# Two edits in a two-layer encoder: the inverse standard deviation by logarithm and exponential, and one accumulation pool for expansion and down projection

## The chip, the cores and the metric

The kernel runs on one core of a Trainium2 chip. The metric is the device time of one execution in microseconds (us). Before the change the median of three executions is 2300.8 us (2297.95 to 2302.07). A change of 0.2% is 4.6 us.

The engines that matter are TensorE (PE: matrix products, with the loading of weights into it listed apart as PEld), VectorE (DVE), ScalarE (ACT), and the transfers (DMA), which SyncE (SP) issues. TensorE writes its sums into PSUM, a small memory of eight banks; DVE and ACT read them from there.

## The reference, cut to what matters

Two layers act on 1056 tokens (1024 of a prompt and 32 of a sample, sharing the weights), with a model width of 1024 and an inner width D_FF of 2816:

```
x <- LN(alpha * x + mixer(x))
x <- LN(alpha * x + SwiGLU(x))              # (silu(x @ w1) * (x @ w3)) @ w2
x <- x + (p[i] @ W_ple) * sigmoid(x @ W_gate)

def layer_norm(x, g, b, eps=1e-5):
    mu = jnp.mean(xf, -1, keepdims=True)
    var = jnp.mean(jnp.square(xf - mu), -1, keepdims=True)
    return ((xf - mu) * lax.rsqrt(var + eps) * g + b)
```

The mixers (causal pooling and a gated convolution in layer 0, a token MLP and a state-space scan in layer 1) are not touched by the change. Everything is float32.

## The kernel before

**Arithmetic.** A float32 product is made of three reduced-precision products: each operand is split into a high part (an ACT copy, line 93 for weights and 411 for activations) and a low part (a DVE subtraction, lines 94 and 412), and high*high, low*high and high*low are accumulated. So every weight that a DMA brings costs one ACT and one DVE instruction before TensorE may use it.

**Stages of a layer.** The mixer; `tail`, which makes the output projection (lines 314 to 316) in token chunks of 384, 384 and 288 and normalises each chunk (first norm of the layer), then the first units of the expansion; `up`, the expansion by w1 and w3; `final`, the down projection by w2 (line 1448); `embed`, which makes the embedding products (line 1555), the gate's products (line 1576) and the second norm, in two token halves of 528.

**The expansion.** The 2816 inner columns are worked in groups g. For each g and each of w1 and w3 there is a *block* of seven outer products in place of eight (a one-level Strassen scheme, `mixed`). An outer product is 24 matmuls of 264 columns (line 1236) into a *quad*, a PSUM tile of two banks. From g = 3 on, in 32 blocks (eight g, w1 and w3, two layers), one of the seven outer products, number 2 for w1 or 4 for w3, is itself made by seven *inner pieces* of six matmuls each (`within`, from line 1140; matmuls at line 1153). Inner pieces 1, 6, 7, 4 use one bank, called u (tile `ia`), and pieces 2, 5, 3 another, called v (tile `ib`). After each piece a DVE addition (line 1164) or an ACT copy (line 1162) takes its sum out; pieces 6, 7, 4 and 3 then go on accumulating into a bank that has been read and is kept. The block's order is fixed by generator steps: pieces 1 and 2, then 5 and 6, then 3 and 7, then 4, with outer products asked for in between.

**PSUM.** `up` has a pool of its own: three quads (`q`) and the tiles `ia` and `ib`, 3*2 + 1 + 1 = 8 banks. It is closed after `up`, and a new pool of four quads is opened for `final` and `embed`. `final` takes all four quads at once (its first four are the four row blocks of one output product). Tiles of a pool are recycled in turn, and a wait for a tile's earlier reader is kept for the tile as a whole.

**The norm.** `norm` (line 1647) is cut into steps, each of which is put off by an amount of TensorE work, so that it runs while products go on: `first` (mean), `second` (variance, then the ACT square root at line 1685), `third` (DVE reciprocal at line 1690, ACT square at 1691), `fourth` and `fifth` (one Newton step at lines 1697 to 1703), then four `pieces` of two of the eight feature blocks (DVE multiplication at line 1709, ACT scale and shift at 1711, then the split 411/412). `minus` (line 1673) subtracts the mean from two feature blocks. There are ten norms in all: three chunks and two halves in each layer.

**The order of the work.** The program is written in one order, and a scheduler with its own model of durations then sets the order of instructions on each engine; on the chip every engine takes its instructions strictly in that order, and waits by semaphores.

Of the kernel before, what the change touches and what calls it, by code (L numbers as in the profile page):

```python
# [9 lines left out]
AF = mybir.ActivationFunctionType  # L10
ALU = mybir.AluOpType
PSUM = bass.MemoryType.PSUM
# [21 lines left out]
LN_A, LN_B, LN_C, LN_D, LN_S = 4.0, 2.0, 2.0, 4.0, 1.0  # L34
# [250 lines left out]
class Kernel:  # L285
# [50 lines left out]
    def build(self):  # L336
        nc, tc, a = self.nc, self.tc, self.a
        with ExitStack() as ctx:
            const = ctx.enter_context(tc.tile_pool(name="const", bufs=1))
            dram = ctx.enter_context(tc.tile_pool(name="dram", bufs=1, space=DRAM))  # L340
            ring = ctx.enter_context(tc.tile_pool(name="ring", bufs=1, side="right"))
            self.w = Weights(nc, ring, plan(a, self.steps, self.ple, self.inner))

            self.const = const
            self.operand("in")

            mp = ctx.enter_context(ExitStack())
            self.mp = mp.enter_context(tc.tile_pool(name="mix0", bufs=1, reuse_waits="tile"))
            xraw = self.mp.tile([P, KD, T], F32, tag="yf", name="xraw")


            xin = a["xT"]
            (t0, n) = CH[0]
            nc.sync.dma_start(out=xraw[:, 0:2, t0:t0 + n], in_=xin[:, 0:2, t0:t0 + n])
            self.w.prefetch()
            for c, (t0, n) in enumerate(CH):
                for k in range(0 if c else 2, KD, 2):
                    nc.sync.dma_start(out=xraw[:, k:k + 2, t0:t0 + n], in_=xin[:, k:k + 2, t0:t0 + n])
            cst = const.tile([P, 3 * P + 64], F32, name="cst")
            nc.sync.dma_start(out=cst, in_=a["cst"])  # L360
            self.ident, self.tri, self.ones = (cst[:, i * P:(i + 1) * P] for i in range(3))
            self.inv = cst[:, 3 * P:3 * P + 64].rearrange("p (g t) -> p g t", g=4)
            prm = const.tile([P, 124], F32, name="prm")
            nc.sync.dma_start(out=prm, in_=a["prm"])
            self.ln = prm[:, 0:64].rearrange("p (l s m) -> p l s m", l=4, s=2)
            self.pscale = prm[:, 64:68]
            self.cw = prm[:, 68:80].rearrange("p (k m) -> p k m", k=3)
            self.scw = prm[:, 80:112].rearrange("p (k m) -> p k m", k=4)
            self.scb = prm[:, 112:120]
            self.nw = prm[:, 120:124]  # L370
            self.mhalf = const.tile([P, 8], F32, name="mhalf")
            nc.vector.memset(self.mhalf, -0.5)
            nc.vector.tensor_scalar(out=self.ones, in0=self.ones, scalar1=1.0 / D, scalar2=None, op0=ALU.mult)
            for c in range(3):
                for k in range(0, KD, 2):
                    self.split(self.x[c], slice(k, k + 2), xraw[:, k:k + 2, CH[c][0]:CH[c][0] + CH[c][1]])

            self.spill = dram.tile([P, KD, T], F32, name="spill")
            self.resid = dram.tile([P, KD, T], F32, name="resid")
            self.acd = dram.tile([72, P], F32, name="acd")  # L380

            self.hidden = [dram.tile([P, 2, 2, NG, TH], F32, name=f"hidden{i}") for i in range(2)]
            for layer in range(2):
                if layer == 0:
                    self.layer0_mixer(self.x, xraw)
                    mp.close()
                else:
                    self.layer1_mixer(self.x)
                with ExitStack() as stack:
                    self.hp = stack.enter_context(tc.tile_pool(name=f"h{layer}", bufs=1, reuse_waits="tile"))  # L390
                    self.w.temps, self.w.temp_bufs = self.hp, 5
                    self.tail(layer)
                    self.tp = stack.enter_context(tc.tile_pool(name=f"t{layer}", bufs=1, reuse_waits="tile"))
                    with tc.tile_pool(name=f"psu{layer}", bufs=1, space=PSUM, reuse_waits="tile") as self.psum:
                        self.psum_bufs = {"q": 3, "ia": 1, "ib": 1}
                        self.up(layer)
                    self.psum = stack.enter_context(
                        tc.tile_pool(name=f"psb{layer}", bufs=1, space=PSUM, reuse_waits="tile")
                    )
                    self.psum_bufs = {"q": 4}  # L400
                    self.final(layer)
                    self.embed(layer)

# [736 lines left out]
    def within(self, layer, j, g):  # L1140


        nc, q, d, x = self.nc, TH // 2, self.sh, self.inside[j]
        m, t = {2: (0, 0), 4: (1, 0)}[j]
        (w,) = self.w.get(("in", layer, g, j))

        def bank(tag):
            return self.bank(tag)[:, :q]

        def one(ps, i, add):  # L1150
            for k in range(2):
                for c, (p, r) in enumerate(((0, 0), (1, 0), (0, 1))):
                    nc.tensor.matmul(  # L1153
                        ps, w[i][p][:, k * P:(k + 1) * P], x[i][r][:, k, :],
                        start=not add and k == 0 and c == 0, stop=k == 1 and c == 2, skip_group_check=add,
                    )
            self.passed(6 * q)

        def to(a, b, ps, new=False):
            o = d[a][:, m, t * TH + b * q:t * TH + (b + 1) * q]  # L1160
            if new:
                nc.scalar.activation(o, ps, AF.Copy)
            else:
                nc.vector.tensor_tensor(o, o, ps, op=ALU.add)

        u = bank("ia")
        one(u, 1, False)
        to(0, 0, u)
        v = bank("ib")
        one(v, 2, False)  # L1170
        to(0, 0, v)
        yield
        v = bank("ib")
        one(v, 5, False)
        to(1, 1, v, True)
        one(u, 6, True)
        to(0, 1, u)
        yield
        one(v, 3, True)
        to(0, 1, v)  # L1180
        one(u, 7, True)
        to(1, 1, u)
        yield
        one(u, 4, True)
        to(1, 0, u, True)
        yield
# [460 lines left out]
    def norm(self, ln, c, S, acc, x, n, done, wait=LN_A, rows=None):  # L1647
# [3 lines left out]
        nc, lp = self.nc, self.hp if rows else self.lp  # L1651
        if rows:
            mean, var, inv, tmp = (r[:, :n] for r in rows[:4])
        else:
# [3 lines left out]
            var, tmp = S[0][:, 1, :], S[0][:, 0, :]  # L1658
# [12 lines left out]
        def minus(k):  # L1671
            z = acc[:, k:k + 2, :]
            nc.vector.tensor_tensor(z, z, mean.unsqueeze(1).to_broadcast([P, 2, n]), op=ALU.subtract)
# [7 lines left out]
        def second():  # L1681
            ps, cut = average(S[1])
            nc.vector.tensor_tensor(cut(var), ps, cut(tmp), op=ALU.subtract)
            nc.vector.tensor_scalar(out=var, in0=var, scalar1=0.0, scalar2=EPS, op0=ALU.max, op1=ALU.add)
            nc.scalar.activation(tmp, var, AF.Sqrt)
            minus(0)
            self.defer(LN_B, third)

        def third():
            nc.vector.reciprocal(inv, tmp)  # L1690
            nc.scalar.activation(tmp, inv, AF.Square)
            minus(2)
            self.defer(LN_B, fourth)

        def fourth():

            nc.vector.tensor_tensor(tmp, tmp, var, op=ALU.mult)
            nc.scalar.activation(tmp, tmp, AF.Copy, scale=-0.5, bias=1.5)
            minus(4)
            self.defer(LN_B, fifth)  # L1700

        def fifth():
            nc.vector.tensor_tensor(inv, inv, tmp, op=ALU.mult)
            pieces(0)

        def pieces(k):
            ks = slice(k, k + 2)
            z = acc[:, ks, :]
            nc.vector.tensor_tensor(z, z, inv.unsqueeze(1).to_broadcast([P, 2, n]), op=ALU.mult)
            for kk in (k, k + 1):  # L1710
                nc.scalar.activation(
                    acc[:, kk, :], acc[:, kk, :], AF.Identity,
                    scale=self.ln[:, ln, 0, kk:kk + 1], bias=self.ln[:, ln, 1, kk:kk + 1],
                )
            if k == 0:
                minus(6)
            self.split(x, ks, z)
            done[c] += 1
            if k + 2 < KD:
                self.defer(LN_D if rows else LN_C, lambda: pieces(k + 2))  # L1720
# [118 lines left out]
```

## Time and profile before

| what | value |
|---|---|
| median of the executions shown | 2300.8 us (2297.95 to 2302.07) |
| profiled execution, own time | 2300.83 us |
| profiled execution, span of its trace | 2298.6 us |
| TensorE busy | 2270.4 us (99%) |
| VectorE busy | 1736.9 us (76%) |
| ScalarE busy | 1060.7 us (46%) |
| data moved | 241.46 MB, mean 105 GB/s |

A row of the profile's groups reads: line, engine, operation, output<-input with shapes, number of instructions | busy us, mean ns of one | idle time of the engine just before them, and what ended it. A row of the waits reads: engine, what it was to write and its line <- the engine, tensor and line that it waited for: total us, times, longest us. A row of the windows reads: from:to, length, then the busy time (and number) of PE, PEld, DVE, ACT, POOL, the granted TensorE clock (1.00 is full), the DMA share and GB/s. A row of the timeline reads: start, duration, engine, line, operation, count, and in brackets the idle time before it and its releaser.

### The profile page before, as it was taken

How to read it: one execution, taken by the hardware profiler on the slowest of the kernel's cores; microseconds unless marked ns; L12 is line 12 of the kernel's file. 1: busy time of each engine (PE TensorE's matmuls, PEld its weight loads, DVE VectorE, ACT ScalarE, POOL GpSimd, SP SyncE). 2: the span in 40 equal slices, each digit the busy share in tenths (PEclk: the TensorE clock that was granted, in tenths of full speed). 3: DMA queues.
4: the chain of work that ended last, by engine and by line, in shares of the span. 5: the costliest groups of instructions: out<-in, count | busy, mean ns of one | idle time of the engine just before them, and what ended most of it. 6: DMA issues, size and time to landing. Idle time of an engine off the chain costs nothing.

```text
span 2298.6 us, 41143 instructions
## 1 busy us (share of the span) xinstructions
PE 2270.4 (99%) x17183; PEld 2236.8 (97%) x17183; DVE 1736.9 (76%) x2820; ACT 1060.7 (46%) x1783; POOL 32.5 (1%) x40
## 2 busy tenths in 40 slices
PE   9999999999999999999999999999999999999998
PEld 8999989999999999999999989999999999999998
DVE  8755798977776788896656774898977776888893
ACT  5432464434443443584542662464444443434581
POOL 0000000000000000000000120000000000000000
PEclk9999999999999999999999999999999999999999
DMA  4113133333334632034211222142332335631132
GB/s 143 55 56 113 56 140 102 107 116 107 107 116 162 255 121 70 28 102 139 84 38 57 102 67 72 38 154 96 123 111 94 112 107 204 256 106 42 47 105 91
DMA packets 96478, 241.46 MB, mean 105 GB/s; under 512 B 12092, under 2 KB 21508, under 8 KB 94244
## 3 DMA queue, kind: packets, MB, share of 16 engines
q1 hardware_dynamic: 95524, 238.15, 30.5%
q8 instruction: 134, 2.20, 0.4%
q10 hardware_dynamic: 768, 0.68, 0.1%
q14 instruction: 52, 0.43, 0.1%
HBM read 196.99 MB, written 41.81 MB: 104 GB/s over the span
## 4 chain that ended last, share of the span: by engine, by line
PE 88%; DVE 7%; DMA 2%; ACT 2%; issue 1%; SPq 0%; POOL 0%; POOLq 0%; ACTq 0%
PE q L1236 28%; PE q L1448 20%; PE q L1576 8%; PE mm L314 6%; PE mm L315 6%; PE mm L316 6%; PE ia L1153 4%; PE ib L1153 3%; PE q L1555 2%; DVE bf L99 1%; PE mm L727 1%; PE mm L728 1%; PE mm L729 1%; DVE w L94 1%; DMA raw<-w 1%; PE ms L863 1%
## 5 line engine op out<-in xcount | busy, mean ns | idle before, releaser
L1448 PE MATMUL q<-w 128*128 128x264 f32 x3696 | 459.1, 286 | 4.3 <-DVE c_all L1254 2.2
L1448 PEld LDWEIGHTS q<-w 128*128 128x128 f32 x3696 | 457.8, 189 | 4.9 <-ACT w L93 4.7
L93 ACT ACTIVATE w<-bf 128x512 fp32r<-128x512 f32 (+1 forms) x314 | 184.5, 626 | 190.2 <-issue 69.1
L94 DVE TENSOR_TENSOR w<-raw,w 128x512 fp32r<-128x512 f32 (+2 forms) x182 | 171.2, 946 | 97.7 <-ACT w L93 97.5
L94 DVE TENSOR_TENSOR w<-bf,w 128x512 fp32r<-128x512 f32 (+1 forms) x314 | 207.0, 687 | 37.7 <-ACT w L93 37.3
L93 ACT ACTIVATE w<-raw 128x512 fp32r<-128x512 f32 (+2 forms) x182 | 149.1, 828 | 163.9 <-PE mm L316 75.2
L314 PE MATMUL mm<-xhgate,w 128*128 128x384 f32 (+1 forms) x576 | 188.6, 327 | 4.7 <-ACT xhgate L411 4.7
L1236 PE MATMUL q<-xhin,w 128*128 128x264 f32 x1152 | 188.3, 285 | 0.6 <-ACT u L481 0.6
L316 PE MATMUL mm<-xlgate,w 128*128 128x384 f32 (+1 forms) x576 | 186.6, 325 | 0.8 <-DVE xlgate L412 0.8
L315 PE MATMUL mm<-xhgate,w 128*128 128x384 f32 (+1 forms) x576 | 187.1, 325 | 0.0
L1576 PE MATMUL q<-xhgate,w 128*128 128x264 f32 x1024 | 167.1, 285 | 0.0
L1236 PEld LDWEIGHTS q<-xhin,w 128*128 128x128 f32 x1152 | 159.5, 188 | 1.5 <-ACT u L481 0.8
L1576 PEld LDWEIGHTS q<-xhgate,w 128*128 128x128 f32 x1024 | 142.0, 188 | 0.3
L314 PE MATMUL mm<-xhin,w 128*128 128x384 f32 (+1 forms) x384 | 127.4, 332 | 7.8 <-ACT xhin L411 5.6
L315 PE MATMUL mm<-xhin,w 128*128 128x384 f32 (+1 forms) x384 | 126.1, 329 | 0.6 <-DVE w L94 0.6
L316 PE MATMUL mm<-xlin,w 128*128 128x384 f32 (+1 forms) x384 | 125.7, 329 | 0.1
L1236 PE MATMUL q<-xhgate,w 128*128 128x264 f32 x768 | 125.3, 285 | 0.3 <-ACT xhgate L1204 0.2
L1236 PE MATMUL q<-t3sum,w 128*128 128x264 f32 x960 | 124.3, 285 | 0.0
L1236 PE MATMUL q<-t1sum,w 128*128 128x264 f32 x960 | 124.0, 285 | 0.0
L1236 PE MATMUL q<-t2sum,w 128*128 128x264 f32 x960 | 123.6, 284 | 0.0
L1236 PEld LDWEIGHTS q<-t1sum,w 128*128 128x128 f32 x960 | 120.3, 189 | 0.0
L1236 PEld LDWEIGHTS q<-t3sum,w 128*128 128x128 f32 x960 | 120.0, 189 | 0.0
(431 smaller groups left out, 4801.9 us busy)
## 6 DMA issues: line engine op xcount, KB each, us to landing
raw<-w SPq DMA_DIRECT2D x116, 512.0 KB, 3.7
hidden<-c_all SPq DMA_DIRECT2D x72, 264.0 KB, 2.1
rawx<-w SPq DMA_DIRECT2D x64, 256.0 KB, 2.9
raw<-w_gate SPq DMA_DIRECT2D x32, 512.0 KB, 3.6
raw<-w_in SPq DMA_DIRECT2D x16, 512.0 KB, 3.8
raw<-w_out SPq DMA_DIRECT2D x16, 512.0 KB, 3.5
xhdown<-hidden SPq DMA_DIRECT2D x12, 528.0 KB, 13.6
resid<-stream SPq DMA_DIRECT2D x4, 1056.0 KB, 4.9
```

The source lines that it names most:

```text
L93: self.nc.scalar.activation(hi, x, AF.Copy)
L94: self.nc.vector.tensor_tensor(lo, x, hi.bitcast(F32), op=ALU.subtract)
L99: self.nc.vector.tensor_tensor(t, a, b, op=op)
L314: nc.tensor.matmul(ps, wh, xh, start=first, stop=False)
L315: nc.tensor.matmul(ps, wl, xh, start=False, stop=False)
L316: nc.tensor.matmul(ps, wh, xl, start=False, stop=last)
L727: nc.tensor.matmul(o, xh, hi[:, s], start=k == 0, stop=False)
L1153: nc.tensor.matmul(ps, w[i][p][:, k * P:(k + 1) * P], x[i][r][:, k, :], start=not add and k == 0 and c == 0, stop=k == 1 and c == 2, skip_ ...
L1236: nc.tensor.matmul(ps[:, a, :TH // 2], w[q][:, ks], x[r][:, k, a * TH // 2:(a + 1) * TH // 2], start=not add and k == 0 and j == 0, stop=k ...
L1448: nc.tensor.matmul(ps[m][:, a, :TH // 2], v[q][:, ms], x[r][:, a * TH // 2:(a + 1) * TH // 2], start=j == 0 and n == 0, stop=j == NG - 1 a ...
L1555: nc.tensor.matmul(ps[:, b, :TH // 2], w[q][:, o:o + P], pe[k][r][:, t * TH + b * TH // 2:t * TH + (b + 1) * TH // 2], start=k == 0 and i ...
L1576: nc.tensor.matmul(ps[:, b, :TH // 2], w[q][:, ks], token_half((self.xh, self.xl), k, t, b)[r], start=k == 0 and i == 0, stop=k == KD - 1 ...
```

## The change

Two edits are made together.

1. *One pool.* The pool of four quads that `final` used is now opened before `up`, and both use it. The tiles `ia` and `ib` are gone; `within` takes one quad and uses its two banks as u and v. All seven pieces of an inner product then lie in one tile.
2. *The norm.* `second` now computes ln(var), exp(-0.5 ln(var)) and its square, three ACT activations in a row; the DVE reciprocal is gone. The Newton step follows in `third`, the last multiplication in `fourth`, and there is no `fifth`. The mean's subtractions `minus(4)` and `minus(6)` move from `fourth` and from the first of the `pieces` into the first two `pieces`, each behind that piece's multiplication.

```diff
@@ the program
                     self.tp = stack.enter_context(tc.tile_pool(name=f"t{layer}", bufs=1, reuse_waits="tile"))
-                    with tc.tile_pool(name=f"psu{layer}", bufs=1, space=PSUM, reuse_waits="tile") as self.psum:
-                        self.psum_bufs = {"q": 3, "ia": 1, "ib": 1}
-                        self.up(layer)
                     self.psum = stack.enter_context(
                         tc.tile_pool(name=f"psb{layer}", bufs=1, space=PSUM, reuse_waits="tile")
                     )
                     self.psum_bufs = {"q": 4}
+                    self.up(layer)
                     self.final(layer)
@@ within
-        def bank(tag):
-            return self.bank(tag)[:, :q]
-
@@
-        u = bank("ia")
+        ps = self.quads()
+        u, v = (ps[:, a, :q] for a in range(2))
         one(u, 1, False)
         to(0, 0, u)
-        v = bank("ib")
         one(v, 2, False)
         to(0, 0, v)
         yield
-        v = bank("ib")
         one(v, 5, False)
@@ norm
-            nc.scalar.activation(tmp, var, AF.Sqrt)
+            nc.scalar.activation(tmp, var, AF.Ln)
+            nc.scalar.activation(inv, tmp, AF.Exp, scale=-0.5)
+            nc.scalar.activation(tmp, inv, AF.Square)
             minus(0)
             self.defer(LN_B, third)

         def third():
-            nc.vector.reciprocal(inv, tmp)
-            nc.scalar.activation(tmp, inv, AF.Square)
+
+            nc.vector.tensor_tensor(tmp, tmp, var, op=ALU.mult)
+            nc.scalar.activation(tmp, tmp, AF.Copy, scale=-0.5, bias=1.5)
             minus(2)
             self.defer(LN_B, fourth)

         def fourth():
-
-            nc.vector.tensor_tensor(tmp, tmp, var, op=ALU.mult)
-            nc.scalar.activation(tmp, tmp, AF.Copy, scale=-0.5, bias=1.5)
-            minus(4)
-            self.defer(LN_B, fifth)
-
-        def fifth():
             nc.vector.tensor_tensor(inv, inv, tmp, op=ALU.mult)
             pieces(0)
@@ pieces
-            if k == 0:
-                minus(6)
+            if k < 4:
+                minus(k + 4)
             self.split(x, ks, z)
```

The scheduler sets a new order from this, which the diff does not show. Line numbers of the changed program are six or so lower: 1153 becomes 1148, 1164 becomes 1159, 1162 becomes 1157, 1236 becomes 1230, 1448 becomes 1442, 1685 becomes 1679.

**TensorE in a block with inner pieces.** Rows at line 1153 (before) or 1148 (after) are the inner pieces, the other rows are outer products; a count behind a row stands for so many matmuls. Before, for a w1 block, from piece 5 on (`ib` with an inner sum), through piece 6 (`ia`), 24 outer matmuls, piece 3 (five rows at `ib`) and piece 7 (`ia`):

```order
L1153 MATMUL ib_4787<-inner_3945,w_4586 128x264 [waits DVE_49]
L1153 MATMUL ib_4787<-inner_3945,w_4586 128x264 x5
L1153 MATMUL ia_4739<-inner_3945,w_4586 128x264 x6
L1236 MATMUL q_4704<-t2sum_3227,w_4701 128x264 [waits Activation_49]
L1236 MATMUL q_4704<-t2sum_3227,w_4701 128x264 x23
L1153 MATMUL ib_4787<-xhin,w_4586 128x264 [waits Activation_49]
L1153 MATMUL ib_4787<-xhin,w_4586 128x264
L1153 MATMUL ib_4787<-xlin,w_4586 128x264
L1153 MATMUL ib_4787<-xhin,w_4586 128x264 x2
L1153 MATMUL ib_4787<-xlin,w_4586 128x264
L1153 MATMUL ia_4739<-inner_3945,w_4586 128x264 [waits DVE_49]
L1153 MATMUL ia_4739<-inner_3945,w_4586 128x264 x5
```

The changed program, for a w3 block, from the last outer matmuls ahead of piece 5 to the first of piece 3:

```order
L1230 MATMUL q_4921<-t2sum_3227,w_4887 128x264 x4
L1148 MATMUL q_4958<-inner_3945,w_4807 128x264 [waits DVE_49]
L1148 MATMUL q_4958<-inner_3945,w_4807 128x264 x5
L1230 MATMUL q_4921<-t2sum_3227,w_4887 128x264 x4
L1148 MATMUL q_4958<-inner_3945,w_4807 128x264 [waits Activation_49]
L1148 MATMUL q_4958<-inner_3945,w_4807 128x264 x5
L1230 MATMUL q_4921<-t2sum_3227,w_4887 128x264 x16
L1148 MATMUL q_4958<-xhin,w_4807 128x264 [waits DVE_49]
```

Before, piece 6 followed piece 5 with no wait. After, all pieces write one tile, q_4958, and each waits for the reader of the piece before it: piece 6 for the ACT copy of piece 5, with four outer matmuls in between. Counted in the same way over the whole block, the outer matmuls between the pieces are, for a w1 block of the changed program, 1 (8) 2 (16) 5 (10) 6 (14) 3 (5) 7 (19) 4, and for a w3 block 1 (20) 2 (8) 5 (4) 6 (16) 3 (9) 7 (15) 4. The reader is an ACT copy behind pieces 5 and 4 and a DVE addition behind the others. All blocks of a kind from g = 3 on repeat this. The number of matmuls is the same in both programs.

**TensorE where the expansion ends and the down projection begins** (layer 0). Before:

```order
L1236 MATMUL q_7639<-t3sum_3228,w_7669 128x264 [waits Activation_49]
L1236 MATMUL q_7639<-t3sum_3228,w_7669 128x264 x23
L1448 MATMUL q_7873<-w_7779 128x264 [waits DVE_49,PE_49,Activation_49]
L1448 MATMUL q_7873<-w_7779 128x264 x5
```

After:

```order
L1230 MATMUL q_7609<-t3sum_3228,w_7639 128x264 [waits Activation_49]
L1230 MATMUL q_7609<-t3sum_3228,w_7639 128x264 x23
L1442 MATMUL q_7837<-w_7747 128x264 [waits PE_49,Activation_49]
L1442 MATMUL q_7837<-w_7747 128x264
L1442 MATMUL q_7837<-w_7747 128x264 [waits DVE_49]
L1442 MATMUL q_7837<-w_7747 128x264 x3
```

Before, the first down matmul waits for the readers of the last expansion product q_7639 (DVE), since the new pool's first quad lies on the old pool's banks. After, the first quad is one that had been read long since; its DVE wait is now for the low part of the weight. The wait for the readers of q_7609 stands at the fourth quad, 36 matmuls later.

**ScalarE in a norm** (first chunk of layer 0). Before:

```order
L1685 ACT_TABLE_LOAD [waits DVE_49]
L1685 ACTIVATE S_0_1_2422<-S_0_1_2422 128x384 [waits Activation_49]
L1691 ACTIVATE S_0_1_2422<-dg_0_0_2492 128x384 [waits DVE_49]
```

After:

```order
L1679 ACT_TABLE_LOAD [waits DVE_49]
L1679 ACTIVATE S_0_1_2422<-S_0_1_2422 128x384 [waits Activation_49]
L1680 ACT_TABLE_LOAD
L1680 ACTIVATE dg_0_0_2492<-S_0_1_2422 128x384 [waits Activation_49]
L1681 ACTIVATE S_0_1_2422<-dg_0_0_2492 128x384 [waits Activation_49]
```

The logarithm and the exponential each come with a load of their function table. Over the program VectorE loses ten instructions (the reciprocals), and ScalarE gains ten activations and twelve table loads.

## The prediction

> **What bounds the kernel now.** I read the page's totals first, then a window over `up` and over two of its blocks, since a stage's limit is not the mean's.
>
> ```profile
> PE 2270.4 (99%) x17183; PEld 2236.8 (97%) x17183; DVE 1736.9 (76%) x2820; ACT 1060.7 (46%) x1783; POOL 32.5 (1%) x40
> 430.00:733.00 303.00, 303.00 (x2484) 303.00 (x2483) 219.62 (x400) 129.68 (x231) 0.00 (x0) 1.00 0.32 110
> 441.60:461.27 19.67, 19.67 (x164) 19.67 (x163) 16.23 (x31) 9.09 (x17) 0.00 (x0) 1.00 0.27 96
> ```
>
> TensorE is busy 99% of the span. In layer 0's inner blocks it has no idle time at all at a clock of 1.00: 303.00 of 303.00 us, 303.00/2484 = 0.122 us a matmul. DVE (219.62) and ACT (129.68) have room. So here any wait put before a matmul lengthens the program one to one, and work taken from DVE or ACT gives nothing. Time can be won only where TensorE does wait, which the list of waits shows:
>
> ```profile
> PE mm L314 <- ACT xhin L411: 5.6, 2, 4.4
> PE mm L314 <- ACT xhgate L411: 4.7, 2, 4.4
> PE q L1448 <- DVE c_all L1254: 2.2, 1, 2.2
> PE q L1448 <- ACT w L93: 2.1, 1, 2.1
> PE q L1555 <- ACT t1down L1560: 0.3, 2, 0.2
> ```
>
> Two of these places belong to the change: 5.6 + 4.7 us at the first norm in `tail`, and 2.2 + 2.1 us where `final` begins.
>
> **Term 1: the inner pieces, +16.8 us.** Each of seven pieces now waits for the reader of the piece before it, because both banks are one tile; the order of the program shows six such waits a block, with few outer matmuls between some. What a round trip costs is read from one passage of the timeline in layer 0 and from the groups:
>
> ```profile
> 649.34 0.90 PE L1153 MATMUL ib<-inner,w 128*128 128x264 f32 x6
> 650.28 0.39 ACT L1162 ACTIVATE c_all<-ib 128x264 f32<-128x264 f32 x1
> ```
>
> ```profile
> L1153 PE MATMUL ib<-inner,w x192: 280/285/317, 432.8 to 1929.2; 128*128 128x264 f32 x192
> L1164 DVE TENSOR_TENSOR s_all<-s_all,ia 128x264 f32<-128x264 f32 x64 | 27.2, 424 | 54.1 <-PE ia L1153 54.1
> L1162 ACT ACTIVATE c_all<-ib 128x264 f32<-128x264 f32 x32 | 12.4, 387 | 2.5 <-PE ib L1153 0.6
> L93 ACT ACTIVATE w<-rawx 128x1024 fp32r<-128x1024 f32 x16 | 16.8, 1048 | 0.0
> L1251 ACT ACTIVATE s_all<-q 128x528 f32<-128x528 f32 x70 | 42.6, 608 | 128.1 <-PE q L1236 128.1
> L94 DVE TENSOR_TENSOR w<-bf,w 128x512 fp32r<-128x512 f32 (+1 forms) x314 | 207.0, 687 | 37.7 <-ACT w L93 37.3
> ```
>
> The six matmuls end at 650.24, the copy starts at 650.28: a hop of 0.04 us. A matmul lasts 0.285 us, the copy 0.39, the DVE addition 0.42. The way back is seen where TensorE waited for ACT in `tail`:
>
> ```profile
> 1490.32 0.44 PE L314 MATMUL mm<-xhgate,w 128*128 128x384 f32 x1 [0.27 <-ACT xhgate L411]
> 1490.60 0.34 PE L315 MATMUL mm<-xhgate,w 128*128 128x384 f32 x1
> 1490.77 0.34 PE L314 MATMUL mm<-xhgate,w 128*128 128x384 f32 x1
> ...
> 1497.49 0.83 ACT L411 ACTIVATE xhgate<-stream0b 128x768 fp32r<-128x768 f32 x1
> 1498.37 0.29 PEld L314 LDWEIGHTS mm<-xhgate,w 128*128 128x128 f32 x1 [4.75 <-ACT xhgate L411]
> 1498.37 0.69 PE L314 MATMUL mm<-xhgate,w 128*128 128x384 f32 x1 [4.43 <-ACT xhgate L411]
> ```
>
> ACT ends at 1498.32 and TensorE goes on at 1498.37: 0.05. There the weights were not loaded ahead (both rows start together). What that costs is seen at full clock at 1490.32: the next matmul starts 0.28 us later where 0.17 is usual, 0.11 more. From the start of a piece's last matmul to the next piece's first useful slot that is 0.285 + 0.04 + 0.39 + 0.05 + 0.11 = 0.88 us by ACT, 0.91 by DVE. With m outer matmuls between, the next would start after (m + 1) * 0.122, so seven or more cover the trip if the reader finds its engine free.
>
> Short by this alone are two waits in a pair of blocks: w1's 3 to 7 (m = 5, 0.73 us: 0.18) and w3's 5 to 6 (m = 4, 0.61 us: 0.27). By a queue ahead of the reader, three more. In w1's 5 to 6 (m = 10, 1.95 us from piece 5's first matmul) ACT has first a copy of 0.61 out of the outer product that ends just before piece 5, then a weight split of 1.05, then the piece's copy. With starts 0.1 us closer than durations, that ends at 0.2 + 0.5 + 0.95 + 0.39 = 2.04, and with 0.16 back it is 2.2: short by 0.3. In w3's 3 to 7 (m = 9) and 2 to 5 (m = 8) a DVE weight split can stand ahead of the addition; DVE is busy 16.23 of 19.67 us in a block, so it often will. One such split of 0.69 us leaves 0.91 + 0.69 against 1.22 and 1.10, short by 0.4 and 0.5 when it has only just begun and by nothing when it is nearly done; I take half of the first, 0.2, and, since behind piece 2 its weight's high part must come from ACT first, 0.1 for the second. The rest have 14 to 20. A pair thus loses 0.18 + 0.27 + 0.3 + 0.2 + 0.1 = 1.05 us; eight groups in two layers are 16 pairs, 16.8. Bounds: readers always at once, 0.45 * 16 = 7.2; at every second of the five short places half a DVE addition of 0.42 more, 16.8 + 16 * 2.5 * 0.21 = 25.2.
>
> The Trainium skill, "PSUM — Partial Sum Buffer", section "PSUM bank collisions raise a hardware error", says that PSUM has to be guarded by bank, so the two banks need no guard between them; by that rule the term would be nothing. The program's order puts the waits there all the same.
>
> **Term 2: the start of `final`, -5.7 us.**
>
> ```profile
> 737.98 3.08 PE L1236 MATMUL q<-t3sum,w 128*128 128x264 f32 x24
> 738.51 2.75 DVE L94 TENSOR_TENSOR w<-t2down,w 128x528 fp32r<-128x528 f32 x4 [0.31 <-ACT w L93]
> 741.80 1.31 DVE L1254 TENSOR_TENSOR c_all<-c_all,q 128x528 f32<-128x528 f32 x2
> 743.26 7.00 PE L1448 MATMUL q<-w 128*128 128x264 f32 x43 [2.20 <-DVE c_all L1254]
> 743.20:747.00 3.80, 3.74 (x19) 3.77 (x20) 3.59 (x6) 0.26 (x1) 0.00 (x0) 0.57 0.97 319
> 1943.20:1947.00 3.80, 3.73 (x30) 3.76 (x31) 3.60 (x6) 0.00 (x0) 0.00 (x0) 1.00 0.97 277
> ```
>
> The new pool's first quad waits for the last expansion product's readers, which stand behind four weight splits on DVE. After, that quad is wanted 36 matmuls, 4.4 us, later, and the first weights' low parts (from 738.51) are mostly there when TensorE comes, at the end of its last outer product near 741.1. Gone are 2.2 and 2.1 us of waits, and in layer 0 the low clock behind it: 19 matmuls in 3.74 us where layer 1 at 1.00 has 30, a loss of 11 * 0.124 = 1.4. Sum -5.7. It is 0 if the low part of the weight arrives as late as the readers did; more than -5.7 there isn't.
>
> **Term 3: the first norm, -2.6 us.**
>
> ```profile
> 1488.67 2.54 DVE L1690 RECIPROCAL dg<-S 128x384 f32<-128x384 f32 x1
> 1494.88 0.95 DVE L1709 TENSOR_TENSOR stream0b<-stream0b,dg 128x768 f32<-128x768 f32 x1
> ...
> 1498.85 0.52 PE L315 MATMUL mm<-xhgate,w 128*128 128x384 f32 x1
> 1499.17 0.52 PE L314 MATMUL mm<-xhgate,w 128*128 128x384 f32 x1
> 296.00:303.00 7.00, 4.59 (x15) 4.37 (x15) 7.00 (x11) 4.71 (x7) 0.00 (x0) 0.54 0.24 75
> 1497.80:1502.00 4.20, 3.63 (x13) 3.55 (x14) 4.20 (x7) 2.86 (x4) 0.00 (x0) 0.59 0.35 125
> L1690 DVE RECIPROCAL dg<-S 128x384 f32<-128x384 f32 x4 | 10.2, 2544 | 0.6 <-ACT S L1685 0.6
> L1685 ACT ACT_TABLE_LOAD x8 | 10.3, 1283 | 5.6 <-DVE S L1684 3.2 <-DVE t3down L1684 2.3
> L1685 ACT ACTIVATE S<-S 128x384 f32<-128x384 f32 x4 | 2.1, 517 | 0.0
> ```
>
> Here DVE is the bound (7.00 of 7.00 us): chunk 1's reciprocal of 2.54 us stands ahead of chunk 0's last piece (1494.88), and TensorE waits 4.4 us for that piece's split. The reciprocal goes, 2.54 us a chunk. In its place ACT gets a second table load and the exponential, 1.28 + 0.52 = 1.80 us, in a row with the first (1.28 + 0.52) and the square, all ahead of the next splits of weights and activations on ACT; and the subtractions of the mean, moved behind the multiplications, lengthen two of the pieces by one DVE instruction of 0.95. 2.54 - 1.80 leaves 0.74 us a chunk on the path, but the chain's waits fall at two places instead of one: I expect stalls of two to two and a half us each where one of 4.4 was, so the same sum of idle time, none of it long enough to bring the clock to 0.54 and 0.59. What that clock costs now: starts 0.32 us apart (1498.85 and 1499.17) where 0.17 is usual, some nine of them, 1.3 us a layer, -2.6 in all. Bounds: the 4.4 shortened by 2.54 too, -7.7; the chunk's two loads wholly on the path of two chunks in each layer, +1.80 * 4 - 2.6 = +4.6.
>
> The Trainium skill, "ScalarE: Activation LUTs", section "Table sets: the hidden batching unit", says that one table set holds both ln and exp, so that one load would do. The built program has a load ahead of each; by the rule, 1.28 us a norm less would stand on ACT, and this term would be near its lower bound.
>
> **Term 4: the second norm in `embed`, +1 us.**
>
> ```profile
> 975.00:1010.00 35.00, 34.83 (x283) 34.48 (x282) 32.92 (x35) 32.10 (x48) 0.00 (x0) 1.00 0.21 65
> L1690 DVE RECIPROCAL t2down<-t2down 128x528 f32<-128x528 f32 x4 | 13.8, 3444 | 0.0
> ```
>
> Here ACT has 32.10 of 35.00 us, and TensorE already waits 0.3 for it. A half adds about 1.28 + 0.65 = 1.9 us to ACT and takes 3.44 from DVE. 1.9 is less than the 2.9 free, so most is covered; I take a quarter of a microsecond for each of four halves. Bounds: 0 and, if all of it shows, 7.7.
>
> **The sum.** Against the execution's own 2300.83 (which is the shown median): 2300.8 + 16.8 - 5.7 - 2.6 + 1 = **2310.3 us**, 0.4% slower. All lower bounds together would give 2300.8 + 7.2 - 5.7 - 7.7 = 2294.6, all upper ones 2338.3; it is unlikely that all lie on one side.
>
> **The rivals.**
> - *A: the readers are in time.* Only the two places of 0.45 us a pair count, 7.2 us, and the gains are as above: 2300.8 + 7.2 - 5.7 - 2.6 + 1 = 2300.7, no change. For it: DVE idles 54.1 us before the addition at line 1164 waiting for TensorE, so readers mostly start at once. Against it: each engine keeps to its order, and the split of 1.05 us stands ahead of the copy in it.
> - *B: faster.* The waits cost nothing, since TensorE's queue or a quicker trip covers four or five matmuls: 2300.8 - 5.7 - 2.6 + 1 = 2293.5. It decides if a trip takes under 0.6 us. Against it: the parts of the 0.88 us are all rows of this trace.
> - *C: ScalarE becomes the bound.* Terms 3 and 4 stand at their upper ends: 2300.8 + 16.8 - 5.7 + 4.6 + 7.7 = 2324. For it: 32.10 of 35.00 us in `embed`. Against it: in `tail` the same window has ACT at 4.71 of 7.00.
> - *D: the gaps lower the clock in `up`.* After gaps of 4.4 us the trace shows 0.54 to 0.59, after 2.1 us once 0.57 and once 1.00. If one in two of the 16 pairs fell to half for as long as after 743 (1.4 us lost), it would be 2310 + 11 = 2321. Against it: the gaps are 0.1 to 0.3 us. The Trainium skill, "TensorE: Matmul & The Clock Gate", section "A second HAM failure mode: psum-queue depth-cycling", tells of such short gaps between groups making the clock oscillate; nothing in this trace shows it for gaps under 2 us.
> - *The change doesn't do what it says*: the order shows the new waits and the absent reciprocals, so I leave this nothing.
>
> **How the numbers follow.** The forecast 0.55, A 0.15, B 0.13, C 0.10, D 0.07. A change of under 0.2% (4.6 us, 2296 to 2305) can't be told from none. Faster: B and a little of A, 0.15. Same: most of A and the forecast's lower edge, 0.2. Slower: the rest, 0.65. The range reaches from A's neighbourhood to between the forecast's upper bound (2310.3 + 8.4 = 2319) and C: 2297 to 2324; B and a little of C and D are left out.
>
> **What would show it.** In the changed profile: idle time of TensorE at the inner pieces' line (now 1148) of 12 to 22 us, in gaps of 0.1 to 0.4, released by DVE at 1159 and ACT at 1157, with the clock at 1.00 there; no wait at line 1442 over 0.5 us near 743 and 1943; no 4.4 us wait at line 314, and clocks over 0.8 behind it; idle in `embed` under 3 us. Gaps at 1148 of under 5 us in all would make the prediction wrong.

## The result, and the profile after

The changed kernel takes 2314.8 us (median, 2313.35 to 2316.38) where the kernel before took 2301.05 beside it: a ratio of 1.0061, 95% interval 1.0048 to 1.0074, so 0.6% slower. The prediction was 2310.3 us, slower, with a range of 2297 to 2324.

The page of the changed kernel gives these totals, and its list of waits begins so:

```profile
span 2312.4 us, 41175 instructions
PE 2285.1 (99%) x17183; PEld 2238.3 (97%) x17183; DVE 1719.8 (74%) x2810; ACT 1086.5 (47%) x1805; POOL 32.5 (1%) x40
...
PE mm L314 <- ACT xhin L409: 3.8, 2, 2.1
PE mm L315 <- DVE w L94: 3.5, 3, 2.3
PE mm L314 <- ACT xhgate L409: 2.9, 2, 2.2
PE ms L1658 <- DVE S L1638: 1.9, 1, 1.9
PE q L1230 <- DVE c L972: 1.8, 2, 0.9
```

VectorE lost 17 us and ScalarE gained 26, TensorE has the same number of instructions and yet 15 us more busy time, and no wait in the list explains that. The loss sits inside the busy time: here a matmul that waits for a few tenths of a microsecond is drawn longer, not preceded by a gap. The window over layer 0's expansion that the prediction quoted, taken again of the changed kernel, shows it by the count of matmuls, and the rows of the inner pieces show it by the idle time of the weight loads (PEld; the first three rows are of the changed kernel, the last is one of the two such rows of the kernel before, which both end in 0.0):

```profile
430.00:733.00 303.00, 302.87 (x2419) 297.16 (x2418) 219.00 (x393) 129.38 (x227) 0.00 (x0) 1.00 0.30 106
...
L1148 PEld LDWEIGHTS q<-inner,w 128*128 128x128 f32 x576 | 75.9, 188 | 12.2 <-ACT c_all L1157 6.5 <-DVE s_all L1159 3.4
L1148 PE MATMUL q<-inner,w x576: 278/285/398, 431.4 to 1950.4; 128*128 128x264 f32 x192
...
L1153 PEld LDWEIGHTS ia<-inner,w 128*128 128x128 f32 x384 | 51.1, 188 | 0.0
```

In the same 303 us TensorE started 2419 matmuls where it had started 2484: 65 fewer, at 0.122 us 7.9 us lost in one layer, at a clock of 1.00 and with "302.87 of 303 busy". The weight loads, which are not stretched (188 ns in both), are idle for 12.2 us ahead of those inner pieces that work on inner sums, where they were idle for 0.0, and the longest matmul there went from 0.317 to 0.398 us.

Stage by stage, measured from the starts of each stage's first and last matmuls in the profiled executions, `embed` from the last matmul of `final` (us; the names of the experiments are explained below):

| stretch | before | after | pool_only | norm_only | shared_tile | pairs | pairs_pool_only |
|---|---|---|---|---|---|---|---|
| start to the end of layer 0's input projection | 186.6 | 184.0 | 184.5 | 186.7 | 185.0 | 185.7 | 186.7 |
| `tail`, layer 0 | 81.8 | 82.5 | 81.1 | 82.2 | 81.6 | 82.5 | 81.7 |
| step from `tail` to `up`, layers 0 and 1 | 0.13, 0.13 | 1.18, 1.18 | 0.13, 0.13 | 1.18, 1.18 | 0.13, 0.13 | 1.18, 1.18 | 0.13, 0.13 |
| `up`, layer 0 | 399.3 | 408.2 | 408.0 | 399.7 | 408.1 | 399.4 | 399.2 |
| `up`, layer 1 | 400.1 | 408.8 | 409.2 | 400.0 | 409.3 | 400.0 | 400.8 |
| step from `up` to `final`, layers 0 and 1 | 2.49, 2.40 | 0.12, 0.12 | 0.12, 0.12 | 2.09, 2.49 | 1.86, 2.86 | 0.12, 0.12 | 0.12, 0.12 |
| `final`, layer 0 | 231.3 | 229.7 | 229.7 | 229.8 | 229.8 | 229.7 | 230.1 |
| `embed`, layer 0 | 119.1 | 119.7 | 119.1 | 120.0 | 119.1 | 119.7 | 119.1 |
| step from `embed` to layer 1 | 0.12 | 0.99 | 0.12 | 0.12 | 0.12 | 0.99 | 0.99 |
| `tail`, layer 1 | 80.6 | 80.6 | 80.7 | 79.4 | 80.7 | 79.2 | 81.5 |
| `embed`, layer 1 | 119.1 | 119.7 | 119.1 | 119.7 | 119.1 | 119.7 | 119.1 |

What the table leaves out (layer 1's mixer, the second `final`) differs by at most 1.5 us. From before to after, `up` loses 8.9 + 8.7 = 17.6 us and the start of `final` gives back 2.4 + 2.3 and 1.5 of clock, 6.2 in all.

One wait is seen in full in a w3 block of layer 0, in the timeline of the changed kernel: piece 5, the copy of its sum, and the weight load and matmuls of piece 6.

```profile
655.20 0.88 PE L1148 MATMUL q<-inner,w 128*128 128x264 f32 x6
656.12 0.39 ACT L1157 ACTIVATE c_all<-q 128x264 f32<-128x264 f32 x1 [0.59 <-PE q L1148]
656.56 0.78 PEld L1148 LDWEIGHTS q<-inner,w 128*128 128x128 f32 x6 [0.21 <-ACT c_all L1157]
656.56 0.99 PE L1148 MATMUL q<-inner,w 128*128 128x264 f32 x6
```

Piece 5 ends at 656.08, the copy runs to 656.51, piece 6 starts at 656.56. Its six matmuls take 0.99 us where the six before it took 0.88, and its weight load starts together with its first matmul: 0.11 for weights that were not loaded ahead. Without the wait it would have started five matmuls after piece 5's last, near 656.41: 0.15 + 0.11 = 0.26 us lost, 0.27 had been forecast.

At the end of the expansion (timeline of the changed kernel) the down projection follows with no wait; the two additions that it used to wait for run while it goes on:

```profile
746.10 3.07 PE L1230 MATMUL q<-t3sum,w 128*128 128x264 f32 x24
749.00 3.25 PE L1442 MATMUL q<-w 128*128 128x264 f32 x25
749.32 1.31 DVE L1248 TENSOR_TENSOR c_all<-c_all,q 128x528 f32<-128x528 f32 x2
```

### The profile page after: what moved, and what is told of

The parts are those of the page before. It is cut to its first block, busy times and chain, and to the rows that moved or that the text cites. A ratio compares the mean times of both kernels' runs of the same rounds, so it can differ in the third digit from the quotient of the medians.

```text
span 2312.4 us, 41175 instructions
## 1 busy us (share of the span) xinstructions
PE 2285.1 (99%) x17183; PEld 2238.3 (97%) x17183; DVE 1719.8 (74%) x2810; ACT 1086.5 (47%) x1805; POOL 32.5 (1%) x40
## 4 chain that ended last, share of the span: by engine, by line
PE 88%; DVE 6%; ACT 3%; DMA 2%; issue 1%; POOL 0%; SPq 0%; ACTq 0%; POOLq 0%
PE q L1230 29%; PE q L1442 20%; PE q L1570 8%; PE q L1148 8%; PE mm L315 5%; PE mm L316 5%; PE mm L314 5%; PE mm L725 1%; PE mm L726 1%; PE mm L727 1%; DVE bf L99 1%; DMA raw<-w 1%; DVE w L94 1%; PE ms L861 1%; DMA raw<-w_out 1%
## 5 line engine op out<-in xcount | busy, mean ns | idle before, releaser
L1230 PE MATMUL q<-t2sum,w 128*128 128x264 f32 x960 | 131.7, 285 | 0.0
L1230 PE MATMUL q<-t1sum,w 128*128 128x264 f32 x960 | 129.1, 285 | 0.0
L1230 PEld LDWEIGHTS q<-t2sum,w 128*128 128x128 f32 x960 | 122.9, 188 | 0.0
```

What stands on the lines that cost most here:

```text
L1230: nc.tensor.matmul(ps[:, a, :TH // 2], w[q][:, ks], x[r][:, k, a * TH // 2:(a + 1) * TH // 2], start=not add and k == 0 and j == 0, stop=k ...
```

## The experiments

The theory is that two parts of the pool edit have opposite signs (one tile for all inner pieces costs, the pool that stays open gains), and that the norm adds a little. The rivals are that the norm's burden on ScalarE makes the readers late, that four recycled quads are to blame rather than the shared tile, and that two engines in one tile disturb each other without any wait.

**pool_only** is the diff's first edit without the norm's:

```diff
-                        self.psum_bufs = {"q": 3, "ia": 1, "ib": 1}
-                        self.up(layer)
                     self.psum_bufs = {"q": 4}
+                    self.up(layer)
...
-        u = bank("ia")
+        ps = self.quads()
+        u, v = (ps[:, a, :q] for a in range(2))
```

> The pool edit alone, with the norm as before. Theory (all seven inner pieces in one tile make each wait for the reader of the piece before; the pool that stays open takes the wait at the start of `final` away): the expansion from its first to its last inner piece is 18.0 us longer over both layers, as in the changed kernel (8.6 and 9.4), and the start of `final` 6.2 us shorter, so 2301.0 + 18.0 - 6.2 = 2312.8 us. Rival (the readers are late only because the new norm's activations and table loads burden ScalarE): the inner cost is below half, 2303 us or less.

Measured: 2310.8 us, ratio 1.0044 (1.0032 to 1.0057). `up` is 8.7 and 9.1 us longer and the start of `final` as short as in the changed kernel. So the whole inner cost is there without the new norm, and the rival falls.

**norm_only** is the second edit without the first:

```diff
-            nc.scalar.activation(tmp, var, AF.Sqrt)
+            nc.scalar.activation(tmp, var, AF.Ln)
+            nc.scalar.activation(inv, tmp, AF.Exp, scale=-0.5)
+            nc.scalar.activation(tmp, inv, AF.Square)
...
-            nc.vector.reciprocal(inv, tmp)
...
-            if k == 0:
-                minus(6)
+            if k < 4:
+                minus(k + 4)
```

> The norm edit alone, with both pools as before. Theory: what is left of the changed kernel's loss when the expansion and the start of `final` are taken off, about +0.7 in the tail of layer 0, +1.05 us before the first expansion product of each layer, +0.6 in `embed` of each layer and +0.9 behind it once: 2301.0 + 4.9 = 2306 us, slower by 0.2%. Rival (the new norm gains, as the prediction had it for the tail, -2.6 + 1): 2299.4 us. The waits of 2.2 and 2.1 us at the start of `final` stay under both.

Measured: 2304.0 us, ratio 1.0015 (1.0007 to 1.0024). The norm edit by itself makes the kernel slower by some 3.5 us; the waits at the start of `final` stay (2.09 and 2.49 us from start to start). The waits that matter, in its list:

```profile
PE mm L314 <- ACT xhin L411: 3.8, 2, 2.1
PE mm L314 <- ACT xhgate L411: 3.2, 2, 2.2
PE q L1448 <- ACT w L93: 2.2, 1, 2.2
...
PE q L1448 <- DVE c_all L1254: 1.8, 1, 1.8
PE q L1236 <- DVE c L974: 1.8, 2, 0.9
```

The waits of 4.4 us have become waits of 2.1 and 2.2, as the prediction had it; the last row is a new wait, of which below. The loss is 1.2 us smaller than the 4.9 expected, measured from the median beside it.

**shared_tile** keeps both pools and the norm, and only puts the two banks into one tile:

```diff
-                        self.psum_bufs = {"q": 3, "ia": 1, "ib": 1}
+                        self.psum_bufs = {"q": 3, "iq": 1}
...
-        u = bank("ia")
+        ps = self.psum.tile([P, 2, 512], F32, tag="iq", name=f"iq{layer}{g}{j}", bufs=1)
+        u, v = (ps[:, a, :q] for a in range(2))
```

> The kernel before with one thing changed: the two one-bank tiles of the inner pieces become the two banks of one tile, still in the expansion's own pool with its three quads. Theory (the shared tile is the whole cost): +18.0 us in the expansion and the waits at the start of `final` kept, 2301.0 + 18.0 = 2319 us. Rival (the cost comes from the inner tile taking its turn among four recycled quads): no change, 2301 us.

Measured: 2315.2 us, ratio 1.0068 (1.0053 to 1.0083), `up` longer by 8.9 and 9.2 us, the waits at the start of `final` still there. The shared tile alone carries the cost, without a fourth quad. The whole came out 15.0 us above the kernel beside it where 18.0 were expected; its trace has 1.6 us less ahead of `tail` and 1.5 less in layer 0's `final`, where this edit does nothing.

**pairs** is the changed kernel with the readers moved behind both pieces of a pair:

```diff
         one(u, 1, False)
-        to(0, 0, u)
         one(v, 2, False)
+        to(0, 0, u)
         to(0, 0, v)
         yield
         one(v, 5, False)
-        to(1, 1, v, True)
         one(u, 6, True)
+        to(1, 1, v, True)
         to(0, 1, u)
```

and likewise for 3 and 7. 

> The changed kernel, with the readers of pieces 1 and 2, of 5 and 6, and of 3 and 7 written behind both pieces of the pair, so that the second piece of a pair follows the first with no reader in between; three waits a block are left, each 23 to 25 outer matmuls (2.8 to 3.1 us) behind the piece that is read. Theory (a round trip of about 0.9 us, longer by a queue, is what TensorE stands idle for): the whole 18.0 us go, 2314.8 - 18.0 = 2296.8 us. Rival (the cost is not the waits but the one tile's two banks in use by TensorE and a reader at once): 2314 us, no change, since the readers then read one bank while TensorE goes on elsewhere as before.

Measured: 2298.2 us, ratio 0.9992 (0.9982 to 1.0001). `up` is back at 399.4 and 400.0 us, as before the change, with the same tile and the same readers, and the weight loads wait no more:

```profile
L1148 PEld LDWEIGHTS q<-inner,w 128*128 128x128 f32 x576 | 74.5, 188 | 0.0
```

It is the waits that cost. This run does not put the rival of two engines in one tile to the test, since the rival has no room in either kernel: in the traces of the changed kernel and of `pairs` none of the 224 readers runs while TensorE works on a piece in the same tile. Both banks in one tile are harmless when some 24 matmuls lie between a piece and the next write into the tile.

**pair56** is `pool_only` with only pieces 5 and 6 written as a pair. 

> The run `pool_only` with only pieces 5 and 6 written as a pair. The trace of `pool_only` gives the waits of piece 6 for the copy of piece 5 as 4.7 us (4 outer matmuls between, 18 times 0.26) and 3.6 us (10 between, 14 times 0.26). Theory (each wait is paid by itself): 2310.8 - 8.3 = 2302.5 us. Rival (the time is handed on to the next wait, since the readers are as late there): 2308 to 2311 us.

Measured: 2305.5 us, ratio 1.0016 (1.0007 to 1.0024), against 1.0044 for `pool_only`: 0.28% or 6.4 us by the ratios, and 7.8 us in `up` by the two traces (404.3 and 405.1 us here), where 8.3 were expected. The time itself is 3.0 us above the theory's number and 2.5 below the rival's. The waits from piece 3 to 7 stay at 0.18 and 0.28 us each, so a wait that goes takes its own time with it and little is handed on. By the starts of the pieces' matmuls in the traces the waits of the changed kernel are these (the time that a piece starts later than its matmuls' pitch would have it, weights included):

| wait | outer matmuls between | forecast, us each | measured, us each | times |
|---|---|---|---|---|
| w1, 3 to 7 (DVE), and two such places in each layer's last w3 block | 5 | 0.18 | 0.18 | 18 |
| w3, 5 to 6 (ACT) | 4 | 0.27 | 0.26 | 16 |
| w1, 5 to 6 (ACT, behind a weight split) | 10 | 0.3 | 0.25 | 14 |
| the same in each layer's first w1 block | 13 | | 0.28 | 2 |
| w3, 3 to 7 (DVE, behind a weight split) | 9 | 0.2 | 0.28 | 14 |
| 2 to 5 in w3 and 1 to 2 in w1 (DVE) | 8 | 0.1 (w3 alone) | 0.03 | 30 |
| w3, 1 to 2 (DVE) | 20 | 0 | 0.13 | 16 |

The rows add up to 18.4 us. Four of the 32 blocks, the first w1 block and the last w3 block of each layer, have other counts of matmuls between their pieces than the rest; it is not so that all blocks from g = 3 on repeat one order.

**pairs_pool_only** leaves the norm edit out of `pairs`. 

> The pool edit alone (norm as before), with the pieces written in pairs as in the run `pairs`. Theory: the pool edit's inner cost of 18.0 us goes and its gain at the start of `final` stays, 2310.8 - 18.0 = 2292.8 us, faster than before by 0.3%. Rival (the pairs lose something of their own, which in `pairs` hid behind the norm's gain): 2296 us or more.

Measured: 2295.3 us, ratio 0.9976 (0.9967 to 0.9986); it beats both kernels. That is 2.5 us above the theory's number and 0.7 below the rival's. The inner cost is gone (`up` 399.2 and 400.8 us); in its trace the step from `embed` to layer 1 is 0.87 us longer than in `pool_only` and the two tails are 1.4 us longer, with the clock at 0.50 for 6.8 us in each where `pool_only` has 3.4. It was run again beside two others: 

> `pairs_pool_only` once more, beside the next two on one chip: 2295 us, 0.24% below the kernel before.

Measured: 2295.7 us, ratio 0.9975 (0.9965 to 0.9985).

Two kernels cut the norm edit in two. **pairs_ln_kept** is `pairs` with the mean's subtractions in their old places; **pairs_minus_moved** is `pairs_pool_only` with only these subtractions moved:

```diff
# pairs_ln_kept, against pairs
             nc.vector.tensor_tensor(inv, inv, tmp, op=ALU.mult)
+            minus(4)
             pieces(0)
...
-            if k < 4:
-                minus(k + 4)
+            if k == 0:
+                minus(6)
# pairs_minus_moved, against pairs_pool_only
-            minus(4)
             self.defer(LN_B, fifth)
...
-            if k == 0:
-                minus(6)
+            if k < 4:
+                minus(k + 4)
```

> The run `pairs` with the norm's subtractions of the mean put back to their old places (one ahead of the first piece, one behind it); logarithm, exponential and the missing step stay. Theory (the norm costs by what the logarithm and exponential bring: table loads, and a first expansion quad on the bank that is read last): 2298 us, as `pairs`, with TensorE's wait of 0.9 us before the first expansion product of each layer. Rival (the moved subtractions cost it): 2293 to 2294 us.

> The run `pairs_pool_only` with the two subtractions of the mean moved into the pieces, square root, reciprocal and the five steps kept. Theory (the moved subtractions cost nothing): 2293 us. Rival (they cost what the norm edit loses): 2297 us.

Measured: 2299.9 us (0.9997, 0.9988 to 1.0006) and 2298.7 us (0.9991, 0.9981 to 1.0001), against 0.9976 without any part of the edit. With the subtractions in their old places nothing is won back, and the wait before the expansion is still there (1.11 us from start to start in both layers). The second result lies 1.7 us above even the rival's number, and its profile has 4 us in a place that no edit touches. So it was run once more, with `pairs`:

> `pairs_minus_moved` once more. Its first profile had 23 matmuls at a low clock early in layer 1's expansion, 4 us that no edit touches. Theory (the moved subtractions cost nothing): within 1.5 us of the run before it in this list. Rival (the loss is theirs): 3 us or more above it, with the expansion of layer 1 again 4 us longer.

> `pairs` once more. Theory (the norm edit as a whole loses some 3.5 us, 2 * 1.05 before the expansion, 2 * 0.6 in `embed`, the rest in the tail): 3 to 4 us above the first run of this list. Rival (the stages even out): within 1.5 us of it.

Measured: 2297.0 us (0.9984, 0.9975 to 0.9994) and 2297.8 us (0.9979, 0.9970 to 0.9988), beside 2295.7 without the edit; the 4 us did not return. The moved subtractions were 3.4 us slower by the first pair of medians and 1.3 by the second, within the theory's 1.5; with intervals of 0.1% to either side that cannot be told from nothing. `pairs` is 2.0 us above `pairs_pool_only` by the second pair of medians, between the two expectations. Its two comparisons differ (0.9992 and 0.9979): the norm edit costs between 1 and 4 us by these ratios, and only in `norm_only` is the loss clear of the interval. How much of it each of its places takes differs from run to run: the tail of layer 1, for one, took 79.2 us in `pairs` and 80.6 in the changed kernel.

**five_banks** asks where the norm's new wait before the expansion comes from. In the timeline of the changed kernel it is this:

```profile
340.10 0.45 DVE L972 TENSOR_TENSOR c<-c,mm 128x288 f32<-128x288 f32 x1
340.69 0.73 PE L1230 MATMUL q<-xhin,w 128*128 128x264 f32 x4 [0.89 <-DVE c L972]
```

The first expansion product waits for the reader of the tail's last product. In the built programs the last product lies on PSUM bank 3 before and on bank 0 with the new norm, while the first quad of the next pool always begins at bank 0. The experiment changes one number of `pairs`:

```diff
-            self.psum_bufs = {"mm": 6, "ms": 2}
+            self.psum_bufs = {"mm": 5, "ms": 2}
```

> The run `pairs` with five instead of six PSUM banks for the products of `tail`. By the program's banks the last of these products then lies under the expansion's first quad in layer 0, as in `pairs`, and in layer 1 no longer. Theory (the 1.05 us before the expansion are a coincidence of banks, brought by the order that the new norm gives): the wait stays 1.18 us from start to start in layer 0 and becomes 0.13 in layer 1. Rival (they are VectorE's lateness through the new norm): 1.1 to 1.2 in both layers.

Measured: 1.18 us in layer 0 and 0.13 in layer 1. In its list of waits one of the two is gone:

```profile
PE q L1230 <- DVE c L972: 0.9, 1, 0.9
```

So this wait is a matter of which bank the last product happens to have (in this run bank 0 in layer 0 and bank 4 in layer 1). The time of its single execution (2302.3 us beside 2304.4) says no more.

## Why the prediction was right, point by point

**Term 1, the inner pieces (+16.8): right, in mechanism and size.** `up` lost 17.6 us, and each wait that was worked out from the trip of 0.88 and 0.91 us came out within 0.08 us. The rows of the tail that gave the way back (0.05) and the unhurried weight load (0.11) held in the inner pieces. Missed were 0.13 us for w3's second piece, which was taken as free with 20 matmuls between: in the changed kernel's trace four DVE instructions stand ahead of its reader, from 487.82 to 490.40, and the addition ends at 490.74, 0.07 us before the piece starts. That is the same queue that the prediction had counted at other places. 0.03 against 0.1 at eight matmuls set part of it off. Rivals A and B of the prediction fall by this, and rival D too: in the expansion the clock was 1.00 throughout with a gap of about a quarter of a microsecond every few microseconds. By the Trainium skill, "TensorE: Matmul & The Clock Gate", section "A second HAM failure mode: psum-queue depth-cycling", short idle gaps between groups of matmuls, of a size that it does not give, make the clock oscillate; the gaps here did not.

One sign that the prediction named turned out badly chosen. It wanted 12 to 22 us of idle time of TensorE at line 1148 and called less than 5 us a refutation; TensorE's own rows there show 0.7 us, of which this is one:

```profile
L1148 PE MATMUL q<-inner,w 128*128 128x264 f32 x576 | 92.6, 296 | 0.3
```

Taken by the letter this would speak against the prediction. The waits are in the rows of the weight loads at that line, idle for 13.5 us in all against 0.1 before, and in the 65 missing matmuls.

**Term 2, the start of `final` (-5.7): right, with a caution.** 2.4 + 2.3 us of waits went, and 1.5 us of clock. But the 1.5 are not the change's to promise, and that they came as forecast is luck: a step of 1.9 to 2.9 us stands there six times in the three kernels `before`, `norm_only` and `shared_tile`, and `final` is 1.5 us longer behind two of them only (231.3 in layer 0 of `before`, 231.3 in layer 1 of `norm_only`, elsewhere 229.8).

**Term 3, the first norm (-2.6): wrong in sign.** It measured +0.8 in the two tails and +2.1 in front of the expansion, +2.9. The step that failed is the one from shorter stalls to a better clock, "none of it long enough to bring the clock to 0.54 and 0.59". VectorE did lose 5 us of work in each tail, the 4.4 us stalls did break up into two or three of 1.7 to 2.3 us, and the idle time of TensorE in the two tails stayed much the same (11.3 us before, 12.0 after without the new wait ahead of the expansion). But the clock fell all the same: to 0.50 for 3.4 us in each tail, behind a wait of 2.13 us in layer 0 and two of 2.23 and 2.34 us in layer 1.

```profile
294.40:297.70 3.30, 3.30 (x12) 3.26 (x11) 3.30 (x6) 1.64 (x4) 0.00 (x0) 0.50 0.00 0
1506.00:1509.40 3.40, 3.40 (x12) 3.40 (x12) 3.40 (x6) 0.46 (x1) 0.00 (x0) 0.50 0.54 154
```

The sign "clocks over 0.8 behind it" failed by this. All fourteen traces have such a fall, of 3.4 or 6.8 us at a time, in each of the two tails, with the old norm and with the new. So the slow matmuls stayed: starts 0.25 to 0.6 us apart cost 4.8 and 3.7 us beyond the pitch of 0.175 in the two tails before, 4.2 and 4.1 after; those at the low clock among them cost 3.7 us in all before and 3.0 after, where the forecast wanted none. The windows over layer 0's tail, before and after, give the whole exchange (each to the first expansion matmul, so with the step of 0.13 and 1.18 us):

```profile
259.59:341.49 81.90, 76.13 (x456) 73.56 (x455) 78.17 (x113) 52.75 (x85) 0.00 (x0) 0.96 0.29 105
```

```profile
256.98:340.69 83.71, 76.11 (x457) 72.85 (x455) 73.32 (x113) 60.00 (x93) 0.00 (x0) 0.98 0.29 103
```

4.9 us less on VectorE, 7.3 more on ScalarE, the mean clock 0.98 for 0.96, and 1.8 us longer. Over all traces the two tails together take 161.3 to 164.1 us with the new norm (six traces) and 161.3 to 163.2 with the square root (eight), so the 0.8 is not clear of chance: the tails neither gained nor, as far as can be told, lost. The second part, 1.05 us a layer, was not in the prediction at all: the new order of the tail gave its last product the bank that the expansion needs first.

On the Trainium skill's rule that ln and exp share a set ("ScalarE: Activation LUTs", "Table sets: the hidden batching unit"): the trace has a load ahead of each of them,

```profile
L1679 ACT ACT_TABLE_LOAD x10 | 12.8, 1283 | 6.3 <-DVE S L1678 3.2 <-DVE t3down L1678 3.0
L1680 ACT ACT_TABLE_LOAD x10 | 12.8, 1283 | 0.2
```

so the twenty loads were paid, 25.6 us of ScalarE where eight loads had cost 10.3.

**Term 4, `embed` (+1): right.** 0.6 us in each layer, by the waits for ScalarE at line 1549, 0.3 us before and 1.4 after (`t1down`, two waits of up to 0.7).

**The sum.** 17.6 - 6.2 + 2.9 + 1.2 is 15.5, against 9.5 forecast. Two more things stand beside it. The step from `embed` to layer 1 grew by 0.9 us (the same kind of wait, for the last reader in `embed`, in the changed kernel and in all versions of `pairs`; not taken apart further). And the profiled execution was 2.6 us faster before the end of layer 0's input projection, where no edit is: that stretch takes 184.0 to 188.2 us in the fourteen traces. So the forecast of 2310.3 was 4.5 us low, and term 3 alone was 5.5 too low. By the terms it was 6.0 low (15.5 against 9.5); that the time came out nearer is luck, since the 2.6 us belong to no edit. Rival C, in which ScalarE's share grows, had the direction of that and not the size (+2.9 and +1.2 where it had +4.6 and +7.7).

## What to carry to other kernels

Two PSUM banks joined in one tile are one thing to the waits, in a program that keeps its waits by tile, as this one does: before joining them, count the matmuls between a reader and the next write into the other half, and compare with one full trip (here 0.9 us: the end of the matmul, the reader, the way back, and weights that are not loaded ahead). If they are too few, write the pieces in pairs ahead of both readers; that kept the gain of the open pool and took the cost away, 0.24% below the kernel before. And look for lost time by counts of matmuls in equal windows or by idle weight loads: on an engine shown as 99% busy, waits of a quarter of a microsecond were drawn here as longer matmuls.

## What the runs showed of the hardware that had not been expected

The clock fell after shorter waits than those of 2 to 5 us that the prediction had looked at. In `five_banks`, early in layer 1's expansion, it was 0.51 for 6 us, behind ten microseconds in which the weight loads were idle for 3.3 us, the longest single wait 1.67 us (the fall began at 1579.1, within the last of the three waits shown):

```profile
1577.19 0.55 PEld L1230 LDWEIGHTS q<-xhgate,w 128*128 128x128 f32 x4 [1.67 <-ACT xhgate L1198]
1578.37 0.30 PEld L1230 LDWEIGHTS q<-xlgate,w 128*128 128x128 f32 x2 [0.63 <-DVE xlgate L1199]
1579.66 0.94 PEld L1230 LDWEIGHTS q<-xhgate,w 128*128 128x128 f32 x4 [1.00 <-ACT xhgate L1198]
```

```profile
1570.00:1580.00 10.00, 7.33 (x54) 6.70 (x54) 10.00 (x17) 5.37 (x8) 0.00 (x0) 0.95 0.33 105
1580.00:1586.00 6.00, 6.00 (x28) 5.78 (x28) 5.02 (x9) 1.77 (x3) 0.00 (x0) 0.51 0.01 3
```

`pairs_minus_moved` had the same fall in one profile and not in the next, and single waits of 1.6 to 2.6 us at the start of `final` brought one in two cases of six. So the same wait is now and then followed by a slow stretch that costs 1.5 to 4 us. What decides it was not settled here. The executions on record show that it goes with the time: of the 32 executions of the kernel before that ran beside `pair56`, the four with a mean granted clock of 0.998 took 2297.8 us on average and the four with 0.994 took 2304.6. So a gain of "clock" should not be counted on.
